# Hybrid gMLP and linear-attention layer in float32: the output projection as seven block products instead of eight

## Chip, cores and metric

The kernel runs on one core of a Trainium2 chip. The metric is the device time of one execution in microseconds (us); the kernel before takes 807.65 us, the median of 3 runs (807.18 to 807.71). Engines are named as in the profile: PE (matmul) with PEld (its weight loads), DVE (vector), ACT (scalar), POOL (GpSimd) and SP, which here only issues DMAs.

## What is computed

One decoder layer on x of 1024 tokens by 1024 features, all float32:

```
h     = rmsnorm(x, pre_norm_g)
z     = h @ w_in                      # 1024 x 6160, split into u, v, gate, q, k, v_B, gate_B, low rank
a_out = gelu(u) * (tril(w_s) @ layernorm(gelu(v)) + b_s) * silu(gate)     # chunks of 128 tokens
b_out = rmsnorm_per_head(gated_linear_attention(q, k, v_B, low rank)) * silu(gate_B)
y     = concat(a_out, b_out) @ w_out  # 1024 x 2048 by 2048 x 1024
out   = x + rmsnorm(y, post_norm_g)
```

## The kernel before, in words

**Number format.** Every large product is made of three float32r matmuls. `split` (L101) cuts an operand into a rounded part hi (a cast on ACT, L102) and the rest lo (a subtraction on DVE, L103). `mm3` (L105) adds hi hi, hi lo and lo hi (L107, L108, L109). Weights of the input projection are multiplied by the pre norm's gain while they are split (`split_scaled`, L115, ACT L118 and DVE L119).

**Stages, in order.** First h is normed, transposed and split, eight token tiles of 128, into four tiles `hT` that stay in SBUF (`prep`, L219). Then attention head by head: `block_b` (L150) brings q and k weights, `block_a` (L132) the v and gate weights in granules of one feature tile (tags wh and wl, nine buffers each), `proj_tok` and `proj_col` project, `attend` (L422) runs the recurrence, and its output goes, transposed, into `mixB`, which stays in SBUF. The low-rank weights `w_lr` are prepared inside the token loop (L266) and used at L318. Then the gating branch: v is projected, gelu'd and normed (`norm`, L552: a subtraction and scale per token tile, then the norm's gain on DVE, L559, and its bias on POOL, L562). For each of eight groups, u and gate are projected (96 matmuls) and `gating` (L566) multiplies by the spatial weights (16 float32 matmuls, L571). The results lie in `vn`.

**The output projection** (L610 to L665) takes the two halves of the tokens one after the other. A half holds eight PSUM banks (four token tiles by two column halves). The 16 feature tiles come in four rounds of four. For each feature tile the weights are loaded from w_out (L620), split, and the mixed features are split into `mm`; the first two of these pairs have a buffer of their own, the others use the memory of `hT`. In the last round each token tile is finished as soon as its sums are complete: sum of squares on ACT (L653), the scale (`rsqrt`, L91: DVE L95, POOL L98), multiplication by the post norm's gain (L660), scale and residual (L662), and three DMAs out.

**Order of the work.** The code names engines and tiles; a scheduler fixes each engine's order when the kernel is built, by the order in the code and by a simulated clock, so that an instruction which could already run may go ahead of earlier ones that wait. On the chip each queue, those of DMA issues too, is worked in that fixed order. A tile's memory is given again when its last reader is done.

Of the kernel before, what the change touches and what calls it, by code (L numbers as in the profile page):

```python
# [8 lines left out]
F32 = mybir.dt.float32  # L9
F32R = mybir.dt.float32r  # L10
# [5 lines left out]
P = 128  # L16
# [17 lines left out]
def hybrid_layer(  # L34
# [27 lines left out]
    mixp = ctx.enter_context(tc.tile_pool(name="mixp", bufs=1))  # L62
    hp = ctx.enter_context(tc.tile_pool(name="hp", bufs=1))
# [41 lines left out]
    def mm3(ps, a, b, start, stop):  # L105
        """ps += a^T b, with a and b given as their two parts"""
        nc.tensor.matmul(ps, a[0], b[0], start=start, stop=False)  # L107
        nc.tensor.matmul(ps, a[0], b[1], start=False, stop=False)  # L108
        nc.tensor.matmul(ps, a[1], b[0], start=False, stop=stop)  # L109

    W = 512
    # the pre norm's gain goes into the rows of w_in: one column of it for each k tile
    gain = const.tile([P, KT], F32, name="gain")

    def split_scaled(hi, lo, src, k):  # L115
        """the two parts of src times the gain of k tile k"""
        g = gain[:, k : k + 1]
        nc.scalar.activation(out=hi, in_=src, func=AF.Copy, scale=g)  # L118
        nc.vector.scalar_tensor_tensor(  # L119
            out=lo, in0=src, scalar=g, in1=hi.bitcast(F32), op0=ALU.mult, op1=ALU.subtract  # L120
        )

    def weight_granules(n, shape):
        return [
            (
                wts.tile(shape, F32R, tag="wh", name="wh", bufs=9),
                wts.tile(shape, F32R, tag="wl", name="wl", bufs=9),
            )
            for _ in range(n)
        ]  # L130

    def block_a(cols, before=lambda k2: None):  # L132
        """512 columns of w_in, k tile by k tile: [(hi, lo)] of [P, 512]"""
        got = []
        for k2 in range(KT // 2):
            before(k2)
            raw = wts.tile([P, 2, W], F32, tag="raw", name="raw", bufs=3)
# [7 lines left out]
            for j, (hi, lo) in enumerate(weight_granules(2, [P, W])):  # L145
                split_scaled(hi, lo, raw[:, j], 2 * k2 + j)
                got.append((hi, lo))
        return got

    def block_b(cols):  # L150
        """two times 128 columns of w_in: [(hi, lo)] by k of [P, 256]"""
        got = []
        for k4 in range(KT // 4):
            raw = wts.tile([P, 4, 256], F32, tag="raw", name="raw", bufs=3)
# [5 lines left out]
            for j, (hi, lo) in enumerate(weight_granules(2, [P, 2, 256])):  # L160
                for i in range(2):
                    split_scaled(hi[:, i], lo[:, i], raw[:, 2 * j + i], 4 * k4 + 2 * j + i)
                    got.append((hi[:, i], lo[:, i]))
        return got

# [8 lines left out]
    def proj_tok(ts, blk):  # L174
        """[tok, col] = h[tok tile] @ w, for the token tiles ts"""
# [8 lines left out]
    def proj_col(hf, blk, i):  # L184
        """[col, tok] = (h @ w)^T for the 128 columns i of a block and a half of the tokens"""
# [8 lines left out]
    # v and gate of the first head, and the low-rank weights, wait in slots of the mixed features  # L194
    def slot_b(shape, dt=F32):
        return mixp.tile(shape, dt, tag="mixB", name="mixB", bufs=H)

    v0, sg0 = slot_b([P, NT, DV]), slot_b([P, NT, DV])
    w_lr = slot_b([P, KT, P], F32R)
# [10 lines left out]
    with tc.tile_pool(name="pre", bufs=2) as pre:  # L210
# [8 lines left out]
        def prep(t):  # L219
# [13 lines left out]
            for j, c in enumerate(halves):  # L233
                nc.vector.tensor_scalar_mul(h[:, c], xt[:, c], rstd)
# [8 lines left out]
        g_rows = pre.tile([KT, P], F32, name="g_rows", bufs=1)  # L243
        nc.sync.dma_start(g_rows, pre_g.rearrange("(k p) -> k p", p=P))
        pt = bank()
        nc.tensor.transpose(pt[:, 0:KT], g_rows, ident[0:KT, 0:KT])
        nc.vector.tensor_copy(gain, pt[:, 0:KT])
        prep(0)
        blk = block_a(
            ((C_BV, DV), (C_BG, DV)), lambda k2: load(1) if k2 == 2 else None  # L250
# [4 lines left out]
        lr_raw = pre.tile([P, KT, RANK], F32, name="lr_raw", bufs=1)  # L255
# [3 lines left out]
        for t in range(NT - 2):  # L259
# [6 lines left out]
            if t == 3:  # L266
                # columns by groups of 32: hi, hi, lo, hi
                nc.gpsimd.memset(w_lr.bitcast(F32), 0.0)
                nc.gpsimd.tensor_tensor(
                    out=lr_raw, in0=lr_raw,  # L270
                    in1=gain.rearrange("p (k o) -> p k o", o=1).to_broadcast([P, KT, RANK]), op=ALU.mult,
                )
                for i in (0, 1, 3):
                    nc.scalar.copy(out=w_lr[:, :, 32 * i : 32 * i + RANK], in_=lr_raw)
                nc.gpsimd.tensor_tensor(
                    out=w_lr[:, :, 64 : 64 + RANK], in0=lr_raw,
                    in1=w_lr[:, :, 0:RANK].bitcast(F32), op=ALU.subtract,
                )

# [1 line left out]
    mixB = []  # L281
    with tc.tile_pool(name="gla", bufs=1) as gp:
# [12 lines left out]
        # low-rank weights by groups of 32 rows, to meet lr's parts: hi, lo, hi, hi  # L295
# [14 lines left out]
        # lr by groups of 32 rows: h w_hi twice rounded, h w_lo, and what the rounding left  # L310
        lrT = gp.tile([P, S], F32R, name="lrT")
        for hf in range(2):
# [3 lines left out]
            for k in range(KT):  # L316
                for i, part in enumerate(hT(k, c)):
                    nc.tensor.matmul(  # L318
                        pl, w_lr[:, k], part,
# [11 lines left out]
        def gates(hd, hf):  # L331
            """exp of b - b_ref, b_ref - b, b_last - b and b, feature-major"""
# [6 lines left out]
            # 16 * log_a = min(z, 0) - ln(1 + exp(-|z|))  # L339
# [38 lines left out]
        def qk(hd, got):  # L378
            """q and k of a head, with their decays, in tiles of two chunks"""
# [42 lines left out]
        def attend(hd, t, got, v, sg, cur):  # L422
            """output of one tile of two chunks, and the state after it"""
# [30 lines left out]
            if e == 1:  # L454
# [4 lines left out]
                def out(t=t, og=og, mx=cur["mx"]):  # L459
# [8 lines left out]
                    )  # L468

                later(out, 3)  # L470

        def new_mix():
            mixB.append(slot_b([P, 2, S]))
            return {"mx": mixB[-1]}
# [32 lines left out]
    vnp = ctx.enter_context(tc.tile_pool(name="vnp", bufs=1))  # L507
    vn = [vnp.tile([P, NT, 256], F32, name=f"vn{j}") for j in range(4)]

# [3 lines left out]
    with tc.tile_pool(name="sgu", bufs=1) as sp_:  # L513
        wsr = vnp.tile([P, G, P], F32, tag="wg", name="wsr")
# [5 lines left out]
        bs = sp_.tile([P, G, P], F32, name="bs")  # L520
        nc.gpsimd.dma_start(
            bs.rearrange("p g t -> p (g t)"), row_bc(b_s.rearrange("g t -> (g t)"), G * P)
        )
        stats = sp_.tile([P, NT, 4, 6], F32, name="stats")
        wsT = sp_.tile([P, G, P], F32, name="wsT")
        for i in range(2):
# [8 lines left out]
            if i == 0:  # L535
# [7 lines left out]
                gb = vnp.tile([P, 2, D], F32, tag="wg", name="gb")  # L543
                nc.gpsimd.dma_start(gb[:, 0], row_bc(ln_g, D))
# [36 lines left out]
        for g in range(G):  # L581
            blk = block_b((C_U + g * P, C_G + g * P))
            for i, func in enumerate((AF.Gelu, AF.Silu)):
                for hf in range(2):
# [15 lines left out]
                    if (i, hf) == (1, 0) and g >= 1:  # L600
                        gating(g)
# [89 lines left out]
```

## Time and profile before

| | before |
|---|---|
| median of 3 runs | 807.65 us |
| profiled execution: span, first to last instruction | 805.6 us |
| median above that span | 2.05 us |
| PE busy | 787.2 us (98%) |
| DVE, ACT, POOL busy | 392.8, 336.8, 126.7 us |
| DMA | 58.53 MB, mean 73 GB/s |
| output projection, first to last matmul | 624.8 to 799.0 us |

How to read it: matmuls are pipelined, so the records of neighbours overlap, and their sum is larger than PE's busy time. The profile's time of its own execution is the span; what lies around it, 2.05 us against the median, is taken over unchanged.

### The profile page before, as it was taken

The page shows a single profiled execution, that of the slowest core. Times are in us where ns is not written, and L with a number is a line of the kernel's source. Part 1 is how long each engine was busy: PE and PEld are TensorE (multiplying, and loading weights), DVE is VectorE, ACT ScalarE, POOL GpSimd, SP SyncE. Part 2 cuts the span into 40 slices and gives each one's busy share as a digit, 9 for nine tenths or more (in the row PEclk, how much of TensorE's full clock was granted, in tenths as well). Part 3 has the DMA queues.
Part 4 walks back from the last instruction along what each step waited for, and adds up shares of the span by engine and source line. Part 5 has one row for each costly group of instructions (what it writes and reads, how often), then busy time and mean ns, then how long its engine had stood idle before and what let it go on. Part 6 is the DMA issues. An engine that isn't in the chain of part 4 may idle for free.

```text
span 805.6 us, 10163 instructions
## 1 busy us (share of the span) xinstructions
PE 787.2 (98%) x3865; PEld 656.8 (82%) x3865; DVE 392.8 (49%) x736; ACT 336.8 (42%) x678; POOL 126.7 (16%) x161
## 2 busy tenths in 40 slices
PE   5999999999999999999999999999999999999996
PEld 4888888887888788888888888888888888888885
DVE  4536688337633763342424996233332613663235
ACT  6628567336633763241414315343432512542222
POOL 2341243221222122120001350000000000010001
PEclk9999999999999999999999999999999999999999
DMA  9303101003100310031503011111110333473304
GB/s 285 116 8 111 52 1 54 1 1 111 54 1 1 111 53 1 1 105 52 157 1 105 0 53 53 52 53 53 53 53 8 125 104 104 145 264 115 105 27 156
DMA packets 48913, 58.53 MB, mean 73 GB/s; under 512 B 3864, under 2 KB 38688, under 8 KB 48864
## 3 DMA queue, kind: packets, MB, share of 16 engines
q1 hardware_dynamic: 45488, 49.36, 20.0%
q0 software_dynamic: 2224, 7.47, 3.0%
q10 hardware_dynamic: 1152, 1.05, 0.4%
q8 instruction: 30, 0.49, 0.3%
q14 instruction: 19, 0.16, 0.1%
HBM read 53.68 MB, written 4.19 MB: 72 GB/s over the span
## 4 chain that ended last, share of the span: by engine, by line
PE 93%; ACT 3%; DVE 2%; DMA 1%; issue 1%; POOL 0%; SPq 0%; POOLq 0%; DVEq 0%; ACTq 0%
PE ps L107 29%; PE ps L108 29%; PE ps L109 29%; PE ps L571 2%; PE ps L318 1%; PE ps L464 1%; DMA raw<-in_w_in_dram 1%; PE ps L238 1%; PE ps L413 1%; ACT wh L118 0%; ACT L349 0%; PE ps L403 0%; PE ps L405 0%; ACT L348 0%; DVE b L352 0%
## 5 line engine op out<-in xcount | busy, mean ns | idle before, releaser
L107 PE MATMUL ps<-wh,hT 128*128 128x512 f32 x384 | 152.0, 397 | 2.3 <-ACT hT L102 2.3
L107 PE MATMUL ps<-hT,wh 128*128 128x512 f32 x384 | 150.7, 393 | 0.0
L109 PE MATMUL ps<-wh,hT 128*128 128x512 f32 x384 | 150.7, 393 | 0.0
L108 PE MATMUL ps<-wl,hT 128*128 128x512 f32 x384 | 150.3, 392 | 0.0
L109 PE MATMUL ps<-hT,wl 128*128 128x512 f32 x384 | 149.8, 390 | 0.0
L108 PE MATMUL ps<-hT,wh 128*128 128x512 f32 x384 | 149.6, 390 | 0.0
L108 PE MATMUL ps<-wl,mm 128*128 128x512 f32 x256 | 99.3, 389 | 0.0
L109 PE MATMUL ps<-wh,mm 128*128 128x512 f32 x256 | 99.3, 389 | 0.0
L107 PE MATMUL ps<-wh,mm 128*128 128x512 f32 x256 | 96.2, 389 | 0.0
L119 DVE SCALAR_TENSOR_TENSOR wl<-raw,gain,wh 128x256 fp32r<-128x256 f32 (+1 forms) x144 | 87.1, 654 | 18.2 <-ACT wh L118 18.0
L118 ACT ACTIVATE wh<-raw,gain 128x256 fp32r<-128x256 f32 (+1 forms) x144 | 74.1, 573 | 30.6 <-PE ps L108 14.8
L107 PEld LDWEIGHTS ps<-wh,hT 128*128 128x128 f32 x384 | 72.7, 189 | 17.0 <-ACT hT L102 2.7
L109 PEld LDWEIGHTS ps<-wh,hT 128*128 128x128 f32 x384 | 72.5, 189 | 14.9 <-DVE hT L103 0.5
L109 PEld LDWEIGHTS ps<-hT,wl 128*128 128x128 f32 x384 | 72.1, 188 | 15.0
L103 DVE TENSOR_TENSOR wl<-raw,wh 128x512 fp32r<-128x512 f32 x64 | 42.9, 690 | 84.5 <-ACT wh L102 84.5
L108 PEld LDWEIGHTS ps<-wl,hT 128*128 128x128 f32 x384 | 72.7, 189 | 13.9
L108 PEld LDWEIGHTS ps<-hT,wh 128*128 128x128 f32 x384 | 72.2, 188 | 14.6
L107 PEld LDWEIGHTS ps<-hT,wh 128*128 128x128 f32 x384 | 72.2, 188 | 14.2
L102 ACT CAST wh<-raw 128x512 fp32r<-128x512 f32 x64 | 38.7, 622 | 98.8 <-PE ps L109 74.4
L108 PEld LDWEIGHTS ps<-wl,mm 128*128 128x128 f32 x256 | 48.1, 188 | 10.1
L109 PEld LDWEIGHTS ps<-wh,mm 128*128 128x128 f32 x256 | 48.1, 188 | 9.9
L107 PEld LDWEIGHTS ps<-wh,mm 128*128 128x128 f32 x256 | 48.0, 188 | 9.9
(166 smaller groups left out, 927.8 us busy)
## 6 DMA issues: line engine op xcount, KB each, us to landing
raw<-in_w_in_dram SPq DMA_DIRECT2D x80, 256.0 KB, 3.6
raw<-in_w_out_dram SPq DMA_DIRECT2D x32, 512.0 KB, 4.1
raw<-in_w_in_dram SPq DMA_DIRECT2D x8, 512.0 KB, 3.9
xr<-in_x_dram POOLq DMA_DIRECT2D x8, 512.0 KB, 4.4
xt<-in_x_dram SPq DMA_DIRECT2D x7, 512.0 KB, 5.5
out_dram<-yo SPq DMA_DIRECT2D x8, 256.0 KB, 2.1
out_dram<-yo ACTq DMA_DIRECT2D x8, 128.0 KB, 2.1
out_dram<-yo SPq DMA_DIRECT2D x8, 128.0 KB, 2.4
```

The lines of the kernel that those rows point to most:

```text
L102: nc.scalar.copy(out=hi, in_=src)
L103: (eng or nc.vector).tensor_tensor(out=lo, in0=src, in1=hi.bitcast(F32), op=ALU.subtract)
L107: nc.tensor.matmul(ps, a[0], b[0], start=start, stop=False)
L108: nc.tensor.matmul(ps, a[0], b[1], start=False, stop=False)
L109: nc.tensor.matmul(ps, a[1], b[0], start=False, stop=stop)
L118: nc.scalar.activation(out=hi, in_=src, func=AF.Copy, scale=g)
L119: nc.vector.scalar_tensor_tensor(out=lo, in0=src, scalar=g, in1=hi.bitcast(F32), op0=ALU.mult, op1=ALU.subtract)
L238: nc.tensor.transpose(pt[:, k * P : (k + 1) * P], h[:, kk * P : (kk + 1) * P], ident)
L318: nc.tensor.matmul(pl, w_lr[:, k], part, start=(k == 0 and i == 0), stop=(k == KT - 1 and i == 1),)
L413: nc.tensor.transpose(pt[:, j * P : (j + 1) * P], ks[:, 2 * j : 2 * j + 2].rearrange("p n c -> p (n c)"), ident,)
L464: nc.tensor.transpose(ptv[:, k, i], og[:, i, k * P : (k + 1) * P], ident)
L571: nc.tensor.matmul(pt[:, c], part[:, c], wsT[:, g], start=True, stop=True)
```

## The change

The product of mixed features (token halves by branch halves) and w_out (branch halves by column halves) is computed from seven block products instead of eight, each of 8 feature tiles by 4 token tiles by 512 columns. Four of them need sums of weight blocks. These sums are made and split during the gating stage, one feature tile in each group (`wout_sums`), and written to a DRAM tile `wo_d` from POOL's queue; the products read the finished parts back. Sums of mixed features are made on DVE in the products (`left`). Mixed features of the attention branch go to DRAM too (`mix_d`) and are read back (`first_a` ahead, the others in the products). The output stage's pool `op` lies in memory that h and the gating stage have given up.

Around this: the pre norm's gain moves from the weights to h, as a row broadcast by two matmuls; weight splits become plain and twice as wide (a tag `gr` of four buffers, each holding both parts of two feature tiles of 512 columns or four of 256); the layer norm's gain goes into the evacuation of the gating product, and its bias into the row `q` added there, through two float32 matmuls with a tile of ones; the low-rank weights are laid out after the token loop; `mixB` has three slots. The diff, cut to its core:

```diff
-    def weight_granules(n, shape):
...
+        g = wts.tile([P, 2] + shape, F32R, tag="gr", name="gr", bufs=4)
...
-                split_scaled(hi, lo, raw[:, j], 2 * k2 + j)
+                split(hi, lo, raw)
...
-                nc.vector.tensor_scalar_mul(h[:, c], xt[:, c], rstd)
+                nc.vector.scalar_tensor_tensor(
+                    out=h[:, c], in0=xt[:, c], scalar=rstd, in1=gain[:, c], op0=ALU.mult, op1=ALU.mult
+                )
...
+        nc.scalar.dma_start(g_row, pre_g.rearrange("(o n) -> o n", o=1))
...
+            nc.tensor.matmul(pt, one, g_row[:, j * W : (j + 1) * W], start=True, stop=True)
+            nc.vector.tensor_copy(gain[:, j * W : (j + 1) * W], pt)
...
+        w_lr = [gp.tile([P, 4, P], F32R, tag="sc" + i, name="w_lr", bufs=2) for i in "hl"]
+        for r, w in enumerate(w_lr):
+            nc.gpsimd.memset(w.bitcast(F32), 0.0)
+            src = lr_raw[:, 4 * r : 4 * r + 4]
+            for i in (0, 1, 3):
+                nc.scalar.copy(out=w[:, :, 32 * i : 32 * i + RANK], in_=src)
+            nc.gpsimd.tensor_tensor(
...
+                    if t % 4 == 3:
+                        c = slice((t - 3) * P, (t + 1) * P)
+                        nc.gpsimd.dma_start(
+                            mix_d[2 * hd : 2 * hd + 2, :, c].rearrange("e p c -> p e c"), mx[:, :, c]
+                        )
...
+                    nc.tensor.matmul(
+                        pt, ones, wsT[:, 4 * r : 4 * r + 4].rearrange("p g t -> p (g t)"),
+                        start=True, stop=True,
+                    )
...
-            nc.vector.tensor_tensor(
-                out=vn[j], in0=vn[j], in1=gb[:, 0:1, c].to_broadcast([P, NT, 256]), op=ALU.mult
-            )
-            nc.gpsimd.tensor_tensor(
-                out=vn[j], in0=vn[j], in1=gb[:, 1:2, c].to_broadcast([P, NT, 256]), op=ALU.add
-            )
...
+        def wout_sums(j):
+            b = sp_.tile([P, 4, W], F32, tag="wb", name="wb")
+            hi = sp_.tile([P, 4, W], F32R, tag="wh", name="wh")
+            for i, (row, col) in enumerate(((8, 0), (8, 1), (0, 0), (0, 1))):
+                nc.sync.dma_start(
+                    b[:, i], w_out[(row + j) * P : (row + j + 1) * P, col * W : (col + 1) * W]
+                )
+            def sums():
+                sub = lambda out, a, c: nc.vector.tensor_tensor(out=out, in0=a, in1=c, op=ALU.subtract)
+                sub(b[:, 0], b[:, 1], b[:, 0])
+                sub(b[:, 1], b[:, 3], b[:, 1])
+                sub(b[:, 3], b[:, 3], b[:, 0])
+                sub(b[:, 2], b[:, 2], b[:, 3])
+                for i in range(2):
+                    c = slice(2 * i, 2 * i + 2)
+                    split(hi[:, c], b[:, c].bitcast(F32R), b[:, c])
+                nc.gpsimd.dma_start(wo_d[j, :, :, 0:W].rearrange("i p c -> p i c"), hi.bitcast(F32))
+                nc.gpsimd.dma_start(wo_d[j, :, :, W:].rearrange("i p c -> p i c"), b)
+            return sums
...
+            sums = wout_sums(g)
...
+                    if (i, hf) == (1, 0):
+                        sums()
+                        if g >= 1:
+                            gating(g)
...
+        def right(j, what):
+            if what in sums_at:
+                g = wts.tile([P, 2, 2, W], F32R, tag="gr", name="gr", bufs=4)
+                nc.sync.dma_start(
...
+                return [(g[:, i, 0], g[:, i, 1]) for i in range(2)]
+            raw = raw_tile([2, W])
...
+            hi, lo = granule([2, W])
+            split(hi, lo, raw)
+            return [(hi[:, i], lo[:, i]) for i in range(2)]
+        def product(ps, l, r, first, done=None):
+            held = []
+            for j in range(8):
+                if j % 2 == 0:
+                    b = right(j, r)
+                a = tuple(op.tile([P, 4, P], F32R, tag="a" + i, name="a" + i, bufs=6) for i in "hl")
+                split(*a, left(j, l))
+                held.append((j, a, b[j % 2]))
+                if done and j in (4, 5, 6):
+                    continue
+                for t in range(4):
+                    for i, a, bb in held:
+                        mm3(ps[t], [m[:, t] for m in a], bb, first and i == 0, i == 7, not first)
+                    if done and j == 7:
+                        done(t)
+                held = []
...
+        def finish(hf, t, xr, pieces):
...
+            rsqrt(rstd, ss[hf][t][:, 0:1], ss[hf][t][:, 1:2])
+            for i, c in enumerate(pieces):
+                nc.vector.scalar_tensor_tensor(
...
+                (nc.sync, nc.scalar)[i % 2].dma_start(out[r, c], y[hf][t][:, c])
+        u = [bank() for _ in range(4)]
+        product(u, "a11", "b11", True)
+        for t in range(4):
+            nc.scalar.copy(out=y[0][t][:, C0], in_=u[t])
+        v = [bank() for _ in range(4)]
+        product(v, "s1", "t1", True)
+        for t in range(4):
+            nc.scalar.copy(out=y[1][t][:, C1], in_=v[t])
+        product(u, "s2", "t2", False)
+        for t in range(4):
+            nc.scalar.copy(out=y[0][t][:, C1], in_=u[t])
+        product(v, "s4", "b22", False)
+        for t in range(4):
+            vtt(out=y[0][t][:, C1], in0=v[t], in1=y[0][t][:, C1], op=ALU.add)
+            sum_sq(ss[0][t][:, 1:2], y[0][t][:, C1])
+        product(u, "s3", "t3", False)
+        xrs = [residual(0, t) for t in range(4)]
...
+        v = [bank() for _ in range(4)]
+        product(v, "a12", "b21", True)
+        for t in range(4):
+            vtt(out=y[0][t][:, C0], in0=v[t], in1=y[0][t][:, C0], op=ALU.add)
+            sum_sq(ss[0][t][:, 0:1], y[0][t][:, C0])
+            vtt(out=y[0][t], in0=y[0][t], in1=pog, op=ALU.mult)
+            finish(0, t, xrs[t], (slice(0, D),))
+        xrs = [residual(1, t) for t in range(4)]
+        def done(t):
+            sum_sq(ss[1][t][:, 0:1], u[t])
+            vtt(out=y[1][t][:, C0], in0=u[t], in1=pog[:, C0], op=ALU.mult)
+            finish(1, t, xrs[t], (C1, slice(0, 256), slice(256, W)))
+        product(u, "a22", "-t4", False, done)
```

`left` returns a mixed tile itself (a11, a12, a22) or makes one sum of two on DVE, in place: s1 = a21 + a22, s2 = s1 - a11, s4 = a12 - s2, s3 = a22 - a11. The first index is the token half, the second the branch (1 attention, 2 gating). `sum_sq` is the sum of squares on ACT.

## Rows read from the trace of the kernel before

**Rows 1.** The page: span, and busy time of each engine.

```profile
span 805.6 us, 10163 instructions
PE 787.2 (98%) x3865; PEld 656.8 (82%) x3865; DVE 392.8 (49%) x736; ACT 336.8 (42%) x678; POOL 126.7 (16%) x161
```

**Rows 2.** Waits of PE: total us, times, longest.

```profile
PE ps L246 <- DMA g_rows<-in_pre_norm_g_dram: 4.7, 1, 4.7
PE ps L464 <- DVE og L457: 2.9, 2, 1.5
PE ps L107 <- ACT hT L102: 2.3, 1, 2.3
PE ps L238 <- DVE h L234: 1.6, 1, 1.6
```

**Rows 3.** Busy time by stretches (instructions), last columns: clock, DMA share, GB/s.

```profile
11.00:21.00 10.00, 10.00 (x44) 7.96 (x45) 8.10 (x15) 8.65 (x17) 3.17 (x7) 1.00 1.12 333
...
500.00:624.80 124.80, 124.80 (x601) 105.11 (x600) 41.01 (x75) 46.27 (x74) 0.00 (x0) 1.00 0.15 45
624.80:716.00 91.20, 91.20 (x404) 75.56 (x403) 45.78 (x78) 37.61 (x74) 5.14 (x9) 1.00 0.42 137
716.00:799.00 83.00, 83.00 (x367) 68.44 (x365) 30.04 (x52) 20.39 (x40) 3.96 (x7) 1.00 0.35 119
799.00:805.60 6.60, 0.03 (x1) 0.00 (x0) 2.35 (x5) 0.69 (x2) 0.55 (x1) 0.85 0.22 79
```

**Rows 4.** Tile mm: ns min/median/max, first and last start.

```profile
L107 PE MATMUL ps<-wh,mm x256: 389/389/389, 624.8 to 798.2; 128*128 128x512 f32 x128
...
L109 PE MATMUL ps<-wh,mm x256: 388/389/389, 625.2 to 798.6; 128*128 128x512 f32 x128
```

**Rows 5.** Groups by shape, 624.8 to 799 us: busy us, mean ns.

```profile
L103 DVE TENSOR_TENSOR wl<-raw,wh 128x512 fp32r<-128x512 f32 x57 | 38.0, 690 | 82.5 <-ACT wh L102 82.4
L102 ACT CAST wh<-raw 128x512 fp32r<-128x512 f32 x57 | 34.4, 621 | 91.5 <-PE ps L109 74.4 <-DMA raw<-in_w_out_dram 15.8
...
L662 DVE SCALAR_TENSOR_TENSOR yo<-yo,rstd,xr 128x512 f32<-128x512 f32 x7 | 5.2, 749 | 1.2 <-POOL rstd L98 1.2
```

**Rows 6.** Groups by shape, whole span.

```profile
L119 DVE SCALAR_TENSOR_TENSOR wl<-raw,gain,wh 128x512 fp32r<-128x512 f32 x48 | 37.3, 804 | 11.8 <-ACT wh L118 11.7
...
L559 DVE TENSOR_TENSOR vn<-vn,gb 128x2048 f32<-128x2048 f32 x4 | 9.1, 2281 | 0.0
...
L230 ACT ACTIVATE h<-xt 128x1024 f32<-128x1024 f32 x7 | 7.5, 1075 | 0.1
```

**Rows 7.** Timeline of DVE, the last scale and multiply: start us, us.

```profile
799.85 0.21 DVE L95 TENSOR_SCALAR rstd<-ss 128x1 f32<-128x1 f32 x1 [2.03 <-ACT junk L653]
799.98 0.68 DVE L660 TENSOR_TENSOR yo<-ps,pog 128x512 f32<-128x512 f32 x1
```

**Rows 8.** Timeline of DVE between the two token halves.

```profile
713.16 2.50 DVE L103 TENSOR_TENSOR mm<-vn,mm 128x512 fp32r<-128x512 f32 x4
...
716.89 0.69 DVE L660 TENSOR_TENSOR yo<-ps,pog 128x512 f32<-128x512 f32 x1
```

**Rows 9.** Timeline of ACT at the output stage's entry.

```profile
622.04 0.62 ACT L102 CAST mm<-mixB 128x512 fp32r<-128x512 f32 x1 [0.73 <-PE ps L108]
```

**Rows 10.** DMA issues by line: KB each, median us to landing.

```profile
raw<-in_w_out_dram SPq DMA_DIRECT2D x32, 512.0 KB, 4.1
```

**Rows 11.** Chain that ended last, in order of time: start us, us.

```profile
2.55 6.28 DMA raw<-in_w_in_dram
...
11.59 0.43 PE ps L108
...
469.11 1.78 PE ps L571 x16
```

**Rows 12.** Timeline of POOL and PE around the low-rank product.

```profile
53.60 0.55 POOL L308 MEMSET scm<- 128x512 f32 x1
...
57.31 3.79 PE L318 MATMUL ps<-hT,mixB 128*128 128x512 f32 x16
```

More of the change, by code (lines that the diff above doesn't have):

```diff
@@ L103, in split, with mm3, granule, raw_tile @@
         (eng or nc.vector).tensor_tensor(out=lo, in0=src, in1=hi.bitcast(F32), op=ALU.subtract)
[L105 to L109, printed above, removed]
-    W = 512
[L113 to L120, printed above, removed]
-        )
-    def weight_granules(n, shape):
[L124 to L127, printed above, removed]
-            )
-            for _ in range(n)
-        ]
-    def block_a(cols, before=lambda k2: None):
+    def mm3(ps, a, b, start, stop, goes_on=False):
+        how = {"skip_group_check": True} if goes_on else {}
+        nc.tensor.matmul(ps, a[0], b[0], start=start, stop=False, **how)
+        nc.tensor.matmul(ps, a[0], b[1], start=False, stop=False, **how)
+        nc.tensor.matmul(ps, a[1], b[0], start=False, stop=stop, **how)
+    W = 512
+    def granule(shape):
+        g = wts.tile([P, 2] + shape, F32R, tag="gr", name="gr", bufs=4)
+        return g[:, 0], g[:, 1]
+    def raw_tile(shape):
+        return wts.tile([P] + shape, F32, tag="raw", name="raw", bufs=3)
+    def block_a(cols, before=lambda k2: None, fine=False):
         got = []
@@ L144, in block_a @@
                 c += n
-            for j, (hi, lo) in enumerate(weight_granules(2, [P, W])):
-                split_scaled(hi, lo, raw[:, j], 2 * k2 + j)
-                got.append((hi, lo))
+            hi, lo = granule([2, W])
+            if fine:
+                for j in range(2):
+                    split(hi[:, j], lo[:, j], raw[:, j])
+            else:
+                split(hi, lo, raw)
+            got += [(hi[:, j], lo[:, j]) for j in range(2)]
         return got
@@ L153, in block_b @@
         for k4 in range(KT // 4):
-            raw = wts.tile([P, 4, 256], F32, tag="raw", name="raw", bufs=3)
+            raw = raw_tile([4, 256])
             for i, c0 in enumerate(cols):
@@ L159, in block_b @@
                 )
[L160 to L163, printed above, removed]
+            hi, lo = granule([4, 256])
+            split(hi, lo, raw)
+            got += [(hi[:, j], lo[:, j]) for j in range(4)]
         return got
@@ L242, in hybrid_layer @@
         load(0, 2)
[L243 to L247, printed above, removed]
+        gain = pre.tile([P, D], F32, name="gain", bufs=1)
+        g_row = pre.tile([1, D], F32, name="g_row", bufs=1)
+        nc.scalar.dma_start(g_row, pre_g.rearrange("(o n) -> o n", o=1))
+        one = pre.tile([1, P], F32, name="one", bufs=1)
+        nc.vector.memset(one, 1.0)
+        for j in range(2):
+            pt = bank()
+            nc.tensor.matmul(pt, one, g_row[:, j * W : (j + 1) * W], start=True, stop=True)
+            nc.vector.tensor_copy(gain[:, j * W : (j + 1) * W], pt)
         prep(0)
         blk = block_a(
-            ((C_BV, DV), (C_BG, DV)), lambda k2: load(1) if k2 == 2 else None
+            ((C_BV, DV), (C_BG, DV)), lambda k2: load(1) if k2 == 2 else None, fine=True
         )
@@ L265, in hybrid_layer @@
             prep(t + 2)
-            if t == 3:
-                nc.gpsimd.memset(w_lr.bitcast(F32), 0.0)
-                nc.gpsimd.tensor_tensor(
[L270 to L281, printed above, removed]
+    mix_d = dram.tile([2 * H, P, S], F32, name="mix_d")
+    wo_d = dram.tile([8, 4, P, 2 * W], F32, name="wo_d")
     with tc.tile_pool(name="gla", bufs=1) as gp:
@@ L318, in hybrid_layer @@
                     nc.tensor.matmul(
-                        pl, w_lr[:, k], part,
+                        pl, w_lr[k // 4][:, k % 4], part,
                         start=(k == 0 and i == 0), stop=(k == KT - 1 and i == 1),
@@ L582, in hybrid_layer @@
             blk = block_b((C_U + g * P, C_G + g * P))
+            sums = wout_sums(g)
+            if g == 6:
+                for j in range(4):
+                    nc.sync.dma_start(
+                        first_a[:, j].rearrange("p t c -> p (t c)"), mix_d[j, :, 0:512]
+                    )
             for i, func in enumerate((AF.Gelu, AF.Silu)):
```

179 lines of the change are left out of this document (98 added, 81 removed).

## The prediction

> **What bounds the kernel now.** I read the page's busy table first, then the waits of PE, then busy time by stretches, then groups by shape inside the output stage. The busy table gives PE 98% of an 805.6 us span [rows 1]; a busy PE alone would prove little, since matmul records overlap, so the second view decides: PE waits for others only 11.5 us in the whole span (and once 0.2), 8.6 of it before its matmuls stream and 2.9 at two attention heads [rows 2]. The stretches agree: from 500 us to the last matmul PE is never idle at a granted clock of 1.00, while DVE and ACT are below half, and 6.6 us of tail follow [rows 3]. So time is the number of matmuls times their spacing. The spacing is not the 389 ns mean of one record. In the output stage the first and last L109 matmul start 173.4 us apart with 255 groups of three between: 0.680 us a group, **0.2267 us a matmul** [rows 4].
>
> **Removed: 96 matmuls.** Before, the stage has 3 x 256 = 768 [rows 4]. Seven products of 8 feature tiles x 4 token tiles x 3 are 672. 96 x 0.2267 = **-21.8 us**, as long as PE stays fed. A product lasts 96 x 0.2267 = 21.8 us, one feature tile 2.72 us, one weight granule (two feature tiles) 5.44 us. Everything else is what could stop the feeding.
>
> **DVE and ACT in the products.** A 512-wide split is ACT 0.62 + DVE 0.69, a 512-wide sum or evacuation 0.69, a normalised 512 piece 0.75 [rows 5]; a 2048-wide sum of two SBUF tiles is 2.28 and a 1024-wide ACT pass 1.08, so I put a 1024-wide split at ACT 1.08 + DVE 1.14 [rows 6]. A product on parked weights (t1, t2, t3) needs DVE 8 x (0.69 + 0.69) = 11.0 us; on raw weights with a left sum (b22) 11.0 + 4 x 1.14 = 15.6; ACT at most 8 x 0.62 + 4 x 1.08 = 9.3. The evacuation of a product runs beside the next one: ACT 4 x 0.62 after the first three, DVE 2.8 after the fourth, 5.5 after the fifth. All stay below 21.8. The banks alternate between two sets, so no product waits for the evacuation of the one before it: nothing there, covered by a whole product.
>
> The tight place is the **sixth hand-over**. There DVE adds (0.69), multiplies 1024 wide (1.14), makes the scale (0.21 [rows 7]) and finishes 1024 wide (2 x 0.75 less one start, 1.4) for four token tiles: 13.8 us. The tiles end 0.68 us apart, so this runs from 2.0 before to 11.8 us after the hand-over. Six part buffers let the splits of the first five tiles of product seven be done before it; the lo part of the sixth comes at 11.8 + 0.7 = 12.5, and PE wants it after 4 x 2.72 + 0.68 = 11.6. **+1.0 us**, bounds 0 and 12.1 (second rival).
>
> That splits may be queued ahead of evacuations is seen at the hand-over between the two token halves: four part splits stand on DVE at 713.16, ahead of the last evacuation of the old half at 716.89 [rows 8], and PE has no gap there [rows 3].
>
> **Entry.** Before, two part pairs lay in a buffer of their own; the others used the memory of h, and their first casts start at 622.04, when the last projection lets its first half go [rows 9]. After, all part buffers lie in that memory. If the lo buffers fall on the second half they wait for the last matmul: one DVE pass of 0.69. **+0.7**, bounds 0 and 2.0.
>
> **DMA.** Loads per product: t 4.2 MB, b 2.1, a21 another 2.1 beside t1, residual rows 2.1. The heaviest is product two, 6.3 MB in 21.8 us = 290 GB/s. The fastest stretch read moved 333 GB/s [rows 3], and a granule's slot frees three granules (16.3 us) before the new one is needed, against 4.1 us landing for 512 KB [rows 10]. Nothing, bounded by the third rival.
>
> **Gating stage.** Each of eight groups gains four 256 KB loads, four subtractions (2.8), two 1024-wide splits (ACT 2.2, DVE 2.3) and two writes of 1 MB from POOL's queue. DVE gains 8 x 5.1 = 41 us and loses four 2.28 us gains [rows 6]; POOL loses four long sums and now carries the writes. A group lasts about 23.6 us of PE (96 x 0.2267 plus 1.78 for 16 gating matmuls [rows 11]), in which DVE was a third busy [rows 3]. On SP the loads of the sums stand between the weight loads of neighbouring groups and wait for the previous writes; behind them wait weights wanted a whole group later. Cost 0, covered by that group; bound in the fourth rival.
>
> **Two ones-matmuls, 512 columns of plain float32,** go on PE. The nearest row is the gating matmul, 16 of 128 columns in 1.78 us, 0.111 each [rows 11]; four times the columns gives 0.445, two make **+0.9**. Bounds 0.45 (the float32r spacing) and twice the row's value, 1.8. The Trainium skill ("FP8 and Floating Point Precision", TensorE Precision Notes) counts four passes for true float32; by that the two would take 1.8 us and the total 790.4. The row speaks for about two passes, since a quarter of the columns takes half of the float32r spacing.
>
> **Norm scales off the weights.** ACT and DVE passes over weights get cheaper (DVE 0.80 to 0.69 for 512 [rows 5, 6]), off the path. The token norm's multiply grows by perhaps 0.3 us per half, and a gain row must be broadcast first: two matmuls and two 0.69 copies. The first matmul waits for the weights' DMA anyway, in flight from 2.55 to 8.83 us [rows 11], and one load leaves that queue. **0**, bounds -1.5 and +2. Coarser granules (four of two feature tiles instead of nine of one) give a head's first weights later, but every release still comes 2.7 us or more ahead of need; the 2.9 us of attention waits may go or double: 0, bounds -2.9 and +3. The eight writes of mixed features go on POOL's queue, ahead of small norms of the next tiles; same bounds.
>
> **Low-rank weights** are laid out after the token loop. POOL is at its set-up with a memset of 0.55 at 53.60, and PE wants them at 57.31 [rows 12]: two memsets, small copies and two subtractions fit in 3.7 us unless they queue behind POOL's DMAs. **+0.3**, bounds 0 and 2.
>
> **Tail.** Before, the scale on DVE (799.85) goes ahead of the last multiply (799.98, 0.68 long) [rows 7]. Now the multiply comes first in the code, and POOL's power waits for the scale: 0.68 later. **+0.7**, bounds 0 and 0.8.
>
> **Sum.** -21.8 + 1.0 + 0.7 + 0.9 + 0.3 + 0.7 = -18.2 against the span of 805.6: 787.4. The median of the runs is 2.05 above that span; carried over, **789.5 us**. With the larger bounds taken one or two at a time, without the rivals: 785 to 794.
>
> **Rivals.** *One: every hand-over stalls.* If the engines' orders put all evacuations ahead of the next product's splits, then after PE's last matmul come one evacuation (0.62 to 0.69), a cast 0.62, a subtraction 0.69 and some 0.2 of signals (an estimate), 2.2 us, at the first four; 3.5 at the fifth, 13.1 at the sixth: 25.4, or 24.4 more than forecast, 813.9, **slower than before**. It decides above 18 us of such gaps. Such gaps would be dearer still at a lowered clock: at the start, after PE had been idle, matmuls are 0.43 us apart [rows 11] against 0.2267, the pace of the 1.2 GHz level, though the stretch's mean clock is printed as 1.00 [rows 3]. Against the rival: [rows 8]. Chance 0.06.
> *Two: only the sixth stalls*, all of it ahead of the splits: 12.1 more, 801.6. For it: the finishing stands earlier in the code and its inputs are always ready. Chance 0.13.
> *Three: starved of parked weights.* If 1 MB takes two landings of 4.1 us in a row, 8.2 against 5.44, products two and three lose 22 less the lead of 16.3, five and seven some 5.6 each: 17 more, 806.5; half of it 798. Against: 333 GB/s. Chance 0.07.
> *Four: parking is too slow.* Load 4.1, sums 2.8, splits 3.4, two writes 6.3 (at 333 GB/s) to 16.4 (8.2 each): 16.6 to 26.7 us a group against 23.6; at worst 7 x 3.1 = 22 more, 811. Chance 0.04.
> *Five: no gain shows,* if parts of the products are waits that the trace cannot foretell, 807 to 808. Chance 0.02.
>
> **How the numbers follow.** The forecast has 0.68. Rivals two and three in part carry the range up to 802, the bounds down to 785; left out is some 0.15. About 0.2% (1.6 us) is what a measurement tells from no change. Faster: forecast, two, most of three and half of four, 0.88; same 0.03 (five and strict three); slower 0.09.
>
> **What would show it.** PE matmuls 3865 - 96 and a few; output stage near 154 us instead of 174; no PE wait between products longer than 0.5 us but one near 1 us late in product seven. A PE wait on a cast, a lo part or a parked granule of several us proves a rival; a gap in the gating stage proves the fourth. A matmul spacing other than 0.2267 would break the first term.

## The result: slower, and the profile after

The kernel after takes **814.75 us** (median of 4 runs, 811.51 to 816.81) against 807.63 for the kernel before in the same comparison: ratio **1.0084, interval 1.0057 to 1.0111**. The forecast was 789.5, with a range of 785 to 802. The profile is of the slowest of the four executions, 816.81 us at a mean clock of 0.989 (the others: 816.6 at 0.989, 812.91 and 811.51 at 0.993), and one execution of run 8 below, of six, took 976.03 us at a clock of 0.754 and is in none of that run's numbers.

The page of the kernel after, and the waits of PE (total us, times, longest); they answer to [rows 1, 2]:

```profile
span 815.1 us, 9989 instructions
PE 786.8 (97%) x3776; PEld 644.6 (79%) x3776; DVE 415.6 (51%) x703; ACT 328.6 (40%) x589; POOL 129.2 (16%) x182
```

```profile
PE ps L236 <- DVE h L230: 6.2, 2, 5.2
PE ps L467 <- DVE og L460: 4.2, 2, 2.3
PE ps L562 <- ACT wsT L557: 4.1, 1, 4.1
PE ps L249 <- DMA g_row<-in_pre_norm_g_dram: 2.3, 1, 2.3
PE ps L111 <- ACT ah L105: 2.1, 1, 2.1
PE ps L112 <- DVE stl L106: 0.7, 1, 0.7
```

PE has 89 matmuls fewer and is as busy as before (786.8 against 787.2 us). That is the first thing to see: the matmuls that stayed have become longer, or further apart.

Cut at the same landmarks, the two traces (starts of PE's instructions, us) say where:

| stretch | before | after | change |
|---|---|---|---|
| start to the first low-rank matmul | 57.3 | 61.7 | +4.4 |
| from there to the first gating matmul | 411.6 | 433.0 | **+21.4** |
| first gating matmul to the last group's | 148.6 | 149.9 | +1.3 |
| from there to the first output matmul | 7.2 | 9.6 | +2.4 |
| output projection, first to last start | 173.9 | 152.2 | **-21.6** |
| last matmul's start to the end | 6.9 | 8.6 | +1.7 |

The output projection gave what was forecast. Busy time by stretches (columns as in [rows 3]) shows it fed and at a clock of 1.00, and the lines of its tile (ns min/median/max, first and last start) give the pace: (806.0 - 654.2) / 223 / 3 = 0.2269 us.

```profile
200.00:220.00 20.00, 17.74 (x94) 14.14 (x93) 9.89 (x20) 9.28 (x16) 5.72 (x6) 0.91 0.07 27
280.00:300.00 20.00, 18.02 (x96) 14.18 (x95) 8.33 (x18) 9.35 (x15) 5.81 (x7) 0.91 0.20 67
400.00:420.00 20.00, 15.85 (x57) 11.25 (x56) 12.16 (x22) 7.94 (x12) 1.51 (x2) 0.83 0.66 214
...
495.00:645.00 150.00, 150.00 (x715) 125.25 (x715) 52.29 (x66) 47.70 (x55) 3.57 (x5) 1.00 0.28 92
654.00:807.00 153.00, 152.63 (x672) 126.09 (x672) 92.57 (x137) 57.91 (x107) 7.48 (x12) 1.00 0.55 198
```

```profile
L111 PE MATMUL ps<-gr,ah x224: 387/389/496, 654.2 to 806.0; 128*128 128x512 f32 x112
```

What was lost, 31 us, lies ahead of that stage and after it. Two things stand out. First, the granted clock is below 1.00 in three stretches. In the kernel before it is 1.00 in each of these; the last of them:

```profile
400.00:420.00 20.00, 20.00 (x90) 16.54 (x90) 3.37 (x11) 1.98 (x6) 0.00 (x0) 1.00 0.02 7
```

Second, the records of the input projection are longer than before; here the matmuls in which h stands still and the weights move, before and then after:

```profile
L107 PE MATMUL ps<-wh,hT x384: 387/389/792, 10.8 to 435.6; 128*128 128x512 f32 x192
```

```profile
L111 PE MATMUL ps<-gr,hT x384: 388/394/1415, 14.1 to 461.0; 128*128 128x512 f32 x192
```

5 ns do not look like much. From start to start the matmuls with moving weights went from 0.2267 to 0.2334 us (1152 of them: 7.7 us), those with moving h from 0.2267 to 0.2290 (1152: 2.6 us). That would be 10.4 us for matmuls that the change does not touch. Matched one by one between the two traces it is less: the differences in spacing add up to **8.1 us** when those of over 0.06 us (waits, another order, a lowered clock) are left out. Among the smaller matmuls of the attention heads the spacing grew less, and with moving h hardly at all.

**The stall at 407 us.** PE's and then ACT's timeline (start us, us) in the stage that projects v:

```profile
407.04 1.04 PE L556 MATMUL ps<-ident,wsr 128*128 128x128 f32 x8
412.23 3.78 PE L562 MATMUL ps<-wsT,ones 128*128 128x512 f32 x4 [4.15 <-ACT wsT L557]
```

```profile
405.77 1.05 ACT L105 CAST wh<-wb 128x1024 fp32r<-128x1024 f32 x1 [9.07 <-issue]
406.72 0.65 ACT L550 ACTIVATE vn<-ps 128x256 f32<-128x256 f32 x2
407.26 1.04 ACT L105 CAST wh<-wb 128x1024 fp32r<-128x1024 f32 x1
408.20 2.94 ACT L105 CAST gr<-raw 128x1024 fp32r<-128x1024 f32 x3
411.04 0.66 ACT L550 ACTIVATE vn<-ps 128x256 f32<-128x256 f32 x2
411.57 1.08 ACT L557 COPY wsT<-ps 128x512 f32<-128x512 f32 x2
```

ACT stands idle for 9 us at the cast of the second weight sums. The bracket names no other engine ("issue"), but DVE's timeline shows the sums come late, since they wait for their load:

```profile
405.00 2.15 DVE L608 TENSOR_TENSOR wb<-wb 128x512 f32<-128x512 f32 x3 [2.55 <-DMA wb<-in_w_out_dram]
```

SP holds the load of the second `wb` until the write of the first has left the buffer (SP's waits: L603 on `wo_d`, 58.7 us over seven times). Behind that cast, in ACT's fixed order, stand three weight casts and the copies for which PE waits.

**The start.** DVE's timeline: the second gain copy stands behind the lo parts of weights, and the second half of h behind it. The first large matmul comes at 14.08, against 10.80.

```profile
9.50 1.29 DVE L106 TENSOR_TENSOR gr<-raw,gr 128x512 fp32r<-128x512 f32 x2 [2.58 <-ACT gr L105]
10.71 0.68 DVE L250 COPY gain<-ps 128x512 f32<-128x512 f32 x1
11.31 1.28 DVE L106 TENSOR_TENSOR gr<-raw,gr 128x512 fp32r<-128x512 f32 x2
12.52 0.74 DVE L230 SCALAR_TENSOR_TENSOR h<-xt,ss,gain 128x512 f32<-128x512 f32 x1
```

### The profile page after: what moved, and what is told of

It reads as the page before. It is cut to its first block, busy times and chain, and to the rows that moved or that the text cites. A ratio compares the mean times of both kernels' runs of the same rounds, so it can differ in the third digit from the quotient of the medians.

```text
span 815.1 us, 9989 instructions
## 1 busy us (share of the span) xinstructions
PE 786.8 (97%) x3776; PEld 644.6 (79%) x3776; DVE 415.6 (51%) x703; ACT 328.6 (40%) x589; POOL 129.2 (16%) x182
## 4 chain that ended last, share of the span: by engine, by line
PE 81%; DVE 5%; ACT 5%; DMA 4%; issue 3%; POOL 1%; SPq 0%; POOLq 0%; DVEq 0%; ACTq 0%
PE ps L111 25%; PE ps L112 25%; PE ps L113 25%; PE ps L589 2%; DMA raw<-in_w_in_dram 2%; ACT gr L105 1%; PE ps L321 1%; DMA wo_d<-wb 1%; PE ps L236 1%; DMA wsr<-in_a_w_s_dram 1%; PE ps L467 1%; DVE stl L106 1%; DVE b L355 1%; DVE og L460 1%; DVE y L758 1%
## 5 line engine op out<-in xcount | busy, mean ns | idle before, releaser
L111 PE MATMUL ps<-gr,hT 128*128 128x512 f32 x384 | 154.7, 405 | 0.0
L112 PE MATMUL ps<-gr,hT 128*128 128x512 f32 x384 | 152.9, 399 | 0.0
L113 PE MATMUL ps<-gr,hT 128*128 128x512 f32 x384 | 152.3, 398 | 0.0
L111 PE MATMUL ps<-hT,gr 128*128 128x512 f32 x384 | 152.2, 396 | 0.0
L113 PE MATMUL ps<-hT,gr 128*128 128x512 f32 x384 | 151.6, 396 | 0.0
L112 PE MATMUL ps<-hT,gr 128*128 128x512 f32 x384 | 151.4, 394 | 0.0
L106 DVE TENSOR_TENSOR gr<-raw,gr 128x1024 fp32r<-128x1024 f32 (+1 forms) x64 | 73.3, 1154 | 33.8 <-ACT gr L105 33.8
L111 PE MATMUL ps<-gr,ah 128*128 128x512 f32 x224 | 87.3, 390 | 2.1 <-ACT ah L105 2.1
L112 PE MATMUL ps<-gr,ah 128*128 128x512 f32 x224 | 87.0, 389 | 0.0
L111 PEld LDWEIGHTS ps<-gr,hT 128*128 128x128 f32 x384 | 73.1, 190 | 16.9 <-issue 0.5
L113 PEld LDWEIGHTS ps<-gr,hT 128*128 128x128 f32 x384 | 73.0, 190 | 16.6
L112 PEld LDWEIGHTS ps<-gr,hT 128*128 128x128 f32 x384 | 73.0, 190 | 16.2 <-issue 0.5
L113 PE MATMUL ps<-gr,al 128*128 128x512 f32 x224 | 85.8, 389 | 0.0
L112 PEld LDWEIGHTS ps<-hT,gr 128*128 128x128 f32 x384 | 72.7, 189 | 15.7
L113 PEld LDWEIGHTS ps<-hT,gr 128*128 128x128 f32 x384 | 72.7, 189 | 15.4
L111 PEld LDWEIGHTS ps<-hT,gr 128*128 128x128 f32 x384 | 73.0, 190 | 15.0
L105 ACT CAST gr<-raw 128x1024 fp32r<-128x1024 f32 (+1 forms) x64 | 62.9, 992 | 44.1 <-PE ps L113 28.2
L111 PEld LDWEIGHTS ps<-gr,ah 128*128 128x128 f32 x224 | 42.1, 188 | 11.3 <-ACT ah L105 2.6
L113 PEld LDWEIGHTS ps<-gr,al 128*128 128x128 f32 x224 | 42.1, 188 | 8.8
L112 PEld LDWEIGHTS ps<-gr,ah 128*128 128x128 f32 x224 | 42.1, 188 | 8.6
```

The lines of the kernel that those rows point to most:

```text
L105: nc.scalar.copy(out=hi, in_=src)
L106: (eng or nc.vector).tensor_tensor(out=lo, in0=src, in1=hi.bitcast(F32), op=ALU.subtract)
L111: nc.tensor.matmul(ps, a[0], b[0], start=start, stop=False, **how)
L112: nc.tensor.matmul(ps, a[0], b[1], start=False, stop=False, **how)
L113: nc.tensor.matmul(ps, a[1], b[0], start=False, stop=stop, **how)
```

## Experiments

Four causes were proposed: the pace (theory A: it depends on where the two operands lie in SBUF relative to each other; theory B: on the new weight tiles, which hold both parts; another rival: on the new stages' DMA or engine traffic), the stall at 407 us (C), the start (D), and the lowered clock after waits.

**1 and 2. Only the places, in the kernel before.** No work changes; 64 bytes per partition are left free, once between the weights and the pool above them (the lines stand behind those that open the weights' pool), once below the weights (ahead of them), so that all operands of the large matmuls move together.

```diff
+    padp = ctx.enter_context(tc.tile_pool(name="padp", bufs=1))
+    pad = padp.tile([P, 16], F32, name="pad")
+    nc.vector.memset(pad, 0.0)
```

> The kernel before, with 64 bytes per partition put between the weight buffers and everything behind them, so that h and the mixed parts lie 64 bytes off the weights' place modulo 128, as h does in the changed kernel; nothing else differs. Theory A (the two operands' places in SBUF against each other set a matmul's pace): token-major projections go from 0.2267 to about 0.2334 us a matmul, feature-major ones to about 0.2290, the output stage, whose stationary parts shift too, to about 0.233; in all 10 us or more, 818 to 823. Theory B (the new weight tiles, both parts in one, set the pace): nothing changes, 807.6.

> The kernel before, with the same 64 bytes put ahead of the weights, so that every operand of the large matmuls moves by 64 and none moves against another. Theory A: 0.2267 us everywhere, 807.6. Theory A2 (the place of h itself modulo 128 counts, not its distance to the weights): a pace other than 0.2267 as with the other pad, 818 or more. Theory B: 807.6.

With the gap between them: **821.75 us**, ratio 1.0178 (1.0158 to 1.0198). With the gap below the weights: 807.31, ratio 1.0002 (0.9991 to 1.0012). The output projection of the first, by its tile; before it was 389 ns and 0.2267 us [rows 4], now (812.7 - 634.2) / 255 / 3 = 0.2333:

```profile
L110 PE MATMUL ps<-wh,mm x256: 393/393/398, 634.2 to 812.7; 128*128 128x512 f32 x128
```

So an edit with no work in it but one small memset makes the kernel slower by 14 us, and what counts is the distance between the two operands, not the place of either. The kernel before has neither the new tiles (theory B) nor the new stages' traffic.

**3 and 4. Which distances.** Gaps of 32 and of 128 bytes between weights and pool, one execution each; the edit for 32, and 32 elements for 128:

```diff
-    pad = padp.tile([P, 16], F32, name="pad")
+    pad = padp.tile([P, 8], F32, name="pad")
```

> The kernel before with 32 bytes put between the weights and everything behind. If any difference modulo 128 costs: 0.2334 and 0.2290 again, 818 to 823. If only a difference of 64 bytes does: 0.2267, 807. Something between, or below 0.2267, is possible, since no run showed it.

> The kernel before with 128 bytes there. Theory A, with a period of 128 bytes or a divisor of it: 0.2267 us, 807. If the difference itself counts, not its remainder: 0.233 again.

824.1 and 823.1 us: slower, both. The output projection's tile, first with 32 and then with 128 bytes, gives 0.2333 and 0.2324 us:

```profile
L110 PE MATMUL ps<-wh,mm x256: 395/395/397, 636.4 to 814.9; 128*128 128x512 f32 x128
```

```profile
L110 PE MATMUL ps<-wh,mm x256: 390/393/404, 636.2 to 814.0; 128*128 128x512 f32 x128
```

So a period of 128 bytes, which theory A had in its first form, is out. In the kernel before, the weights, `hT` and `mm` lie multiples of 2048 bytes apart, as the build places them. In the kernel after, `gr` and `hT` are 64 bytes off a multiple of 256 (the slower pace), while `gr` and the part buffers `ah`, `al` are a multiple of 256 apart (0.2269 above). All of it fits 0.2267 at multiples of 256 bytes and a slower pace at the other distances tried.

**5. The distance mended in the kernel after.**

```diff
+    padp = hps.enter_context(tc.tile_pool(name="padp", bufs=1, side="right", reuse_waits="tile"))
+    pad = padp.tile([P, 16], F32, name="pad")
+    nc.vector.memset(pad, 0.0)
```

> The changed kernel, with h moved down by 64 bytes, so that it agrees modulo 128 with the weights; the output stage's tiles stay where they are. Theory A: all 2304 matmuls of the input projection at 0.2267 us, which gives back 1152 x 0.0067 + 1152 x 0.0023 = 10.4 us: 804.3. Theory B: 0.2334 and 0.2290 stay, 814.7. The other losses (start, v stage, two attention heads, entry, tail) stay under both.

**808.33 us** (ratio 1.0011, 1.0001 to 1.0021), the profiled span 805.9: 9.2 less than that of the kernel after. `hT` now lies a multiple of 256 from `gr`, though not one of 512, and the record is 389 ns again:

```profile
L114 PE MATMUL ps<-gr,hT x384: 387/389/1405, 14.6 to 452.1; 128*128 128x512 f32 x192
```

The waits are all still there (the one on `wsT` 4.5, on `og` 4.3). Theory A holds, and theory B is out: the tiles `gr` are the same. Matched one by one as above, the pace gives back 7.8 us, not 10.4; the medians differ by 6.4, and this one is 4 above the expectation.

**6. The sums begin later.** The raw spatial weights take a buffer of the sums' tag, so the first sums can't load before those are transposed.

```diff
-        wsr = sp_.tile([P, G, P], F32, name="wsr")
+        wsr = sp_.tile([P, G, P], F32, tag="wb", name="wsr")
```

> The changed kernel, with the raw spatial weights in the slot of the tile that the first weight sums are made in, so that loading and parking of sums can only begin when these are transposed, at the end of the v stage's first half. Theory C (parking that begins in the v stage holds ACT's queue and with it the copy that PE waits 4.1 us for): the wait is under 0.5 us, no half clock behind it, 4.1 + 3.4 + about 1 less: 806. Rival (the two ones-matmuls wait for their copies wherever the sums stand): a PE wait of 1 us or more stays there, 813 or more.

**807.01 us** (ratio 1.0008, 0.9993 to 1.0022), span 804.6. PE's wait on `wsT` falls from 4.1 to 0.4 us, and between the same matmuls on either side of the stall (401.4 and 428.1 us in the kernel after) the trace is **6.7 us** shorter: more than the wait, because the clock does not fall after it. Theory C holds, though its expectation priced 8.5. The span is 10.5 shorter because this trace also lacks the clock's falls at the second and third head (last section). ACT now has the weight casts as their matmuls free the buffers:

```profile
403.19 0.66 ACT L550 ACTIVATE vn<-ps 128x256 f32<-128x256 f32 x2 [0.35 <-PE ps L113]
403.74 1.08 ACT L557 COPY wsT<-ps 128x512 f32<-128x512 f32 x2
```

The same run prices the two **ones-matmuls** at full clock. They are four instructions, 0.43 us apart (first and last start 404.4 and 405.8):

```profile
L562 PE MATMUL ps<-wsT,ones x4: 592/592/697, 404.4 to 405.8; 128*128 128x512 f32 x4
```

**7. The second gain copy on ACT.**

```diff
-            nc.vector.tensor_copy(gain[:, j * W : (j + 1) * W], pt)
+            (nc.vector.tensor_copy, nc.scalar.copy)[j](gain[:, j * W : (j + 1) * W], pt)
```

> The changed kernel, with the second half of the broadcast gain copied out of PSUM by ACT instead of DVE. Theory D (the start is late because that copy stands on DVE behind the first weights' lo parts, and the second half of h behind it): the first large matmul starts near 11.5 us instead of 14.1, and 2 to 3 us go from the total, about 812. Rival (the two broadcast matmuls, four slow passes on PE until 6.0, make the start late by themselves): it stays at 13 us or more.

811.95 us (two runs; ratio 1.0054, 1.0036 to 1.0071), the first large matmul at 13.12, not 11.5: one of the three us came back. That is the rival's number, but not its mechanism. The next run, with the same edit, shows why: the two broadcast matmuls end at 6.1 us there, and on ACT too the copy stands behind weight casts, and these behind a DMA.

**8. The three edits together.**

> The changed kernel with three mends: h moved by 64 bytes, parking not before the v stage's second half, second gain copy on ACT. If the three losses add: 10.4 + 8 + 2.5 less than 814.7, about 794, faster than the kernel before by 1.6%. If one of them only moves to the next wait: 798 to 803.

Ratio **0.9912 (0.9896 to 0.9927)** to the kernel before, median 800.21, lowest 799.24; the profiled span is 800.2. This is 1% below the kernel before. The spans of 5, 6 and 7 lie 9.2, 10.5 and 4.6 below the kernel after, 24.3 together, and this one 14.9. ACT's timeline at the start, and the waits of PE:

```profile
9.39 1.14 ACT L108 CAST gr<-raw 128x512 fp32r<-128x512 f32 x2 [4.48 <-DMA raw<-in_w_in_dram]
10.44 0.58 ACT L253 COPY gain<-ps 128x512 f32<-128x512 f32 x1
```

```profile
PE ps L239 <- DVE h L233: 4.8, 2, 4.3
PE ps L470 <- DVE og L463: 4.1, 2, 2.1
...
PE ps L114 <- ACT ah L108: 2.1, 1, 2.1
PE ps L114 <- ACT gr L108: 1.3, 2, 1.1
```

A new wait of 1.3 on weight casts has come, and the clock fell after the second head and at the output stage's entry. The 24.3 counts the clock twice: the traces of 6 and 7 each happen to have none of its falls at the heads, over 3 us in both. The edits' own places in the traces give 7.8 (pace), 6.7 (stall) and 1.0 (start), 15.5 together, so the three losses very nearly add. The expectation's 794 was too low because it priced them at 20.9.

**9 and 10. Tail and start.** Both carry the three edits. In the first the scale of a late token tile goes ahead of the multiplication by the post norm's gain (`late`); in the second, besides, the pre norm's gain comes by a DMA to all partitions (the last two lines).

```diff
             rsqrt(rstd, ss[hf][t][:, 0:1], ss[hf][t][:, 1:2])
+            if late:
+                late()
...
-        nc.scalar.dma_start(g_row, pre_g.rearrange("(o n) -> o n", o=1))
...
+        nc.scalar.dma_start(gain, row_bc(pre_g, D))
```

> The three edits together, and in the last token tiles the scale (DVE, then POOL's power) stands ahead of the multiplication by the post norm's gain, which no longer delays it. In the run of the three edits the last matmul starts at 791.40 and the span ends at 800.2: 8.8 us of tail. Theory A, only the last tile's order counts: the scale of the last tile moves up by one multiplication (0.68), tail 8.1, total 0.7 below that run. Theory B, the tail is DVE's backlog, in which each tile's multiplication delays its scale and the scale's wait for POOL delays the next tile's multiplication: the last two tiles gain 0.68 each and a part of POOL's wait, tail 7.2 to 7.5, total 1.3 to 1.6 below. Rival: the end is set by the DMAs out, tail unchanged at 8.8. All else as in that run, about 800 us.

> As the run before in this call, and the pre norm's gain row is brought to all partitions by one DMA in place of a row load, two matmuls with a column of ones and two copies. In the run of the three edits the second gain copy stood on ACT at 10.44 behind two weight casts that waited for their load (9.39), and the first large matmul came at 12.82 against 10.80 before the change. Theory: the gain's copies behind the weights' split are what holds the start; without them the first matmul comes at 10.8 to 11.3 and the total falls by 1.5 to 2. Rival: the 512 KB that the DMA now writes delay the weights by 1.6 us (at the 333 GB/s of the start before), the cast starts at 11.0 and the first matmul comes at 12.4 to 13, no gain. The engines' orders in the attention heads are set anew in this kernel, which may shift the total by a few us either way; the start is read from the first matmul.

The first: **799.42 us**, ratio 0.9895 (0.988 to 0.991). DVE's last pieces end at 793.45, 4.30 us behind the start of the last matmul (789.15), against 5.44 in run 8: 1.1 gained, between the two theories. The end followed by 0.3 alone, since the last DMA took 4.2 us instead of 3.3; in the second run, with the same 4.30, it took 3.1, and the tail was 7.4. So theory B has the mechanism, and a landing that varies by a us hides it. What is left of the backlog stands in DVE's timeline: the last scale waits for the three pieces of the tile before.

```profile
789.52 1.54 DVE L763 SCALAR_TENSOR_TENSOR y<-y,rstd,xr 128x512 f32<-128x512 f32 x3
790.98 0.21 DVE L101 TENSOR_SCALAR rstd<-sums 128x1 f32<-128x1 f32 x1
791.11 0.68 DVE L803 TENSOR_TENSOR y<-ps,pog 128x512 f32<-128x512 f32 x1
791.91 1.54 DVE L763 SCALAR_TENSOR_TENSOR y<-y,rstd,xr 128x512 f32<-128x512 f32 x3
```

The second: 799.93, ratio 0.9907 (0.989 to 0.9923): no gain over the first. The first large matmul comes at 12.10, between the theory's 11.3 and the rival's 12.4. The gain's matmuls and copies are gone. The weights are not late, as the rival had it (first cast at 8.95, 9.39 in run 8), but the first x tile is. Its load now shares the DMA with the gain's 512 KB, which fits the delay but was not tested apart. The tile is squared only at 5.67 (3.47 in run 8):

```profile
5.67 0.63 ACT L225 ACTIVATE h<-xt 128x512 f32<-128x512 f32 x1 [3.16 <-DMA xt<-in_x_dram]
```

## Why the prediction was wrong, point by point

**The term that was forecast is right, the assumption under it is not.** 96 matmuls fewer at 0.2267 gave -21.6 in the output projection, against -21.8. But the sum took 0.2267 as the pace of all the matmuls that stay; the prediction named another spacing as what would break its first term, and priced none. The pace hangs on where the allocator puts two tiles relative to each other (runs 1 to 5), the change moved both, and 2304 untouched matmuls paid some 8 us. No rival had this mechanism.

**"Cost 0, covered by that group" failed at the first groups.** The gating stage itself did hide the sums: 149.9 us against 148.6, no PE wait in it (window 495 to 645), and the 1.3 is the pace. What failed is that the scheduler let the first two groups' sums go ahead into the v stage, where ACT's fixed order put a cast that waited for a parked write ahead of work that PE needed. I had asked of SP's queue what waits behind a delayed load, and found weights wanted much later; I had not asked it of ACT's. The fourth rival had the cause (parking slower than its cover: its writes take 4.7 and 6.5 us) but in the wrong place. The price was 6.7 us (run 6).

**Ones-matmuls: +0.9 forecast, 4 x 0.43 to 0.53 = 1.8 measured.** I read the 16 records of a gating group [rows 11] as 16 matmuls. The code issues eight (two halves by four blocks), so a float32 matmul is two records; a record of 512 columns takes 0.43, one float32r matmul 0.2267. The Trainium skill ("FP8 and Floating Point Precision", TensorE Precision Notes) counts four passes for true float32: two records of about two float32r spacings each agree with it, and the estimate of 1.8 worked out from it was right where my reading of the row was wrong.

**Norm scales: 0 with bounds -1.5 and +2; 3.3 at the first matmul.** I let the weights' DMA cover the gain's broadcast. It covers the matmuls; it can't cover the copies, which stand behind the weights' parts on either engine (runs 7 and 8). The three ways tried put the first matmul at 12.1 to 14.6, never at 10.8.

**Entry: 0.7 forecast, 2.4 measured.** The cause fits (the part buffers lie in memory that the last projection still reads, though the trace can't tell that from ACT's fixed order), but the chain was too short. Behind PE's last matmul ACT works off three things:

```profile
652.14 0.60 ACT L635 ACTIVATE u<-ps 128x512 f32<-128x512 f32 x1 [1.70 <-PE ps L113]
652.63 1.04 ACT L105 CAST gr<-raw 128x1024 fp32r<-128x1024 f32 x1
653.57 2.18 ACT L105 CAST ah<-first_a 128x512 fp32r<-128x512 f32 x4
```

The bound of 2.0 was just too low. Whether that weight cast could stand earlier was not tried.

**Sixth hand-over: +1.0 forecast, nothing measured.** No gap between products at all; the orders set splits between the finishing steps. The first, second and third rivals did not occur: granules of 1 MB landed in 4.8 us, not 8.2.

**Attention waits: 0, bounds -2.9 and +3.** The waits alone stayed inside: 4.2 instead of 2.9 at the heads and 0.7 at `stl`. But between the same matmuls, without the pace, the heads cost 6.3, outside the bound; 3.1 of it is the clock that fell after two of these waits, told below. The prediction had priced a lowered clock in no term of the heads. **Tail: +0.7 forecast, +1.7**, by DVE's backlog.

In sum: -21.6 in the output projection; against it the pace 8.1, the stall in the v stage 6.7, the heads 6.3, the start 3.3, the entry 2.4, the ones-matmuls and their wait 2.3, the tail 1.7, and 0.5 between the first large matmul and the first head. These make up the 31 us of the profiled execution. The kernel with the three edits gets the first two back, and a us of the start, and is 1% faster than before. The chance of slower, 0.09, rested on hand-overs and on parking, none of it on the pace.

## What to carry to other kernels

Before a spacing is carried over to a changed kernel, ask what sets it: it is a measurement of one layout, and a change that moves tiles moves it too, for every matmul of the kernel. If the records of untouched matmuls get a few ns longer, look at the distance of their operands, and move one pool so that it is a multiple of 256 bytes, before looking for contention. And where work is added "beside" a bound engine, ask of every engine's fixed order which instruction may wait there for a DMA, and what that the bound engine needs stands behind it, in the stage before as well as in the one where the code has it.

## What was not expected of the hardware

**The distance of a matmul's two operands in SBUF sets its pace:** 0.2267 us with them multiples of 256 bytes apart, 0.2324 to 0.2333 in the output projection of the kernel before with 32, 64 or 128 more. Which multiples beyond those seen are fast, and what in the chip does it, stays open.

**Short waits cost more than their length, but not each time.** PE's timeline at the second head, in the kernel after and in run 6:

```profile
206.70 0.69 PE L467 MATMUL ps<-ident,og 128*128 128x128 f32 x2 [2.26 <-DVE og L460]
...
207.61 0.63 PE L111 MATMUL ps<-hT,gr 128*128 128x512 f32 x1
208.04 0.63 PE L112 MATMUL ps<-hT,gr 128*128 128x512 f32 x1
```

```profile
205.83 0.44 PE L467 MATMUL ps<-ident,og 128*128 128x128 f32 x2 [1.98 <-DVE og L460]
...
206.34 0.40 PE L111 MATMUL ps<-hT,gr 128*128 128x512 f32 x1
206.58 0.39 PE L112 MATMUL ps<-hT,gr 128*128 128x512 f32 x1
```

After 2.26 us without a matmul the next large ones come 0.43 apart, the pace of the 1.2 GHz level; after 1.98 they come 0.23 apart. The stretch from 192 to 291 us, with this one fall in it, took 99.0 us; the same work in run 6, without it, 97.1, of which 0.3 is the shorter wait. The length of the wait alone does not decide. At the third head of the kernel after the wait is 1.98 too, and here the clock fell, a us later, which cost another 1.5:

```profile
290.97 0.44 PE L467 MATMUL ps<-ident,og 128*128 128x128 f32 x2 [1.98 <-DVE og L460]
...
292.30 0.63 PE L111 MATMUL ps<-hT,gr 128*128 128x512 f32 x1
```

In run 8 the clock fell after 1.91 at the second head and not after 2.15 at the third. Before, waits of 1.4 and 1.5 cost nothing of the kind.
